# Storing tiles 4 and 5 as a pair in a batched x·yᵀ kernel, with VectorE taking half of their evictions and GpSimd half of one rearrangement

## The chip, the core and the metric

One core of a Trainium2 chip. The metric is the device time of one execution in microseconds, as the median of several runs; the kernel before takes 297.76 us (three runs, 297.63 to 298.08).

## The reference

```python
batch, n_heads, seq_t, seq_s, channels = 8, 12, 512, 512, 64
# x: (batch, n_heads, seq_t, channels), y: (batch, n_heads, seq_s, channels), float32
def reference(x, y):
    return np.einsum('bhtc,bhsc->bhts', x, y).astype(np.float32)
```

For each of 96 heads the result is x times y transposed, 512 x 512, contracted over 64 channels. The inputs are 12.6 MB each, the output is 100.7 MB, all float32.

## The kernel before

**Tiles and groups.** The heads are taken in 6 groups of 16. A group's x and its y are one load each of 2 MB (128 partitions of 16 KB): load 2g is x of group g, load 2g + 1 is y. A group gives two *halves* i = 2g and 2g + 1, and each half gives V = 4 output tiles of 2 MB, 48 tiles in all; tile o belongs to half o // 4.

**Slots.** `room` is 8 slots of 16 KB per partition, in 4 pairs: slots 2n and 2n + 1 are pair n. Loads go to slots 0 to 4 (`places`, line 154), and output tiles go through the same slots. Slots 5, 6 and 7 hold, until they are used for output, the bfloat16 copies of groups 1, 2 and 3 (`xks`, `ybs`, lines 78 to 88): x in the first half of the slot, y in the second. `held` (line 157) makes a tile that goes into such a slot wait for the readers of these copies.

**From a load to a tile.**
- `compress(n)` (line 208) turns load n into bfloat16. An x load is one ScalarE instruction. A y load is four instructions, on VectorE, GpSimd, VectorE and ScalarE (`in_front`; the last y load has GpSimd in the last place).
- `mix(i, engine, part)` (line 231) rearranges the x copy of half i into `xb`, four parts; halves 0, 1 and 2 on GpSimd inside the first loop, later ones on VectorE.
- `transposes(i)` (line 246): two VectorE transposes, `xb` to `xT` and the y copy to `yT`. There are two of each, for even and odd halves; the second instruction tells TensorE that a half is ready (`made`).
- `all_products()` (line 280): TensorE goes through all tiles in order. Each tile is two groups of four 128 x 512 matmuls, one into PSUM buffer `pm0` and one into `pm1` (half of PSUM each). A group waits until its buffer was emptied (`free0`, `free1`).
- `result(o)` (line 390): the two evictions of tile o, `pm0` and `pm1` into the two halves of its slot, on ScalarE (on VectorE for the last tile alone), and then `store(o)`.
- `store(o)` (line 365): tiles 0 to 5 (`o < SINGLE`) are each stored with one 2 MB transfer from slot `alone[o]`. From tile 6 on, an even and an odd tile fill one pair, and the odd one issues one 4 MB transfer for both (line 386). Which pair is used follows `ROUNDS`: 1, 0, 2 in turn for ten pairs of tiles, then all four pairs in turn. The pair of tiles 44 and 45 is stored in parts, and tail work (`shares`, `rest`) follows.

**What sets the order.** Each engine runs its instructions in the order in which the program emits them, and waits on semaphores that `emit` derives from the names read and written. All loads and nearly all stores are issued by SP on one hardware queue, in emission order. The first loop (line 430) runs over loads n = 0 to 11; `load(n + 5)` is issued in turn n for n below 5, loads 10 and 11 in turns 6 and 8. Tiles 0 and 1 come after `compress(8)` and `compress(9)`, tiles 2 and 3 ahead of `compress(10)` and `compress(11)`. Then `prepare(2)` (transposes of half 2, x copies of half 3) and the loop of lines 446 to 449 over the other tiles, with a `prepare` after each fourth one.

Of the kernel before, what the change touches and what calls it, by code (L numbers as in the profile page):

```python
# [9 lines left out]
def kernel(  # L10
# [25 lines left out]
    NH = 2 * NG  # L36
    V = G // 4
# [3 lines left out]
    SLOTS = 5  # L41
    N = K * S
    SINGLE = 2 * V - 2
    SHARED = V * NH - V
    PAIRS = 4
    LATE = 10
    ROUND = [1, 0, 2]
    ROUNDS = [ROUND[n % 3] for n in range(LATE)]
    while len(ROUNDS) < (V * NH - SINGLE) // 2:
        ROUNDS += [PAIRS - 1, *ROUND[LATE % 3:], *ROUND[:LATE % 3]]  # L50
    LAST = 2 * ROUNDS[(V * NH - SINGLE) // 2 - 1]
    CUT = [S, 3 * S]
# [39 lines left out]
    pms = [nc.alloc_psum_tensor(f"pm{i}", [P, 4, S], fp32)[:, :, :] for i in range(2)]  # L92
# [6 lines left out]
    def need(name, points, told=True):  # L99

        best = {}
        for p, v in points:
            if known[name].get(p, 0) < v:
                best[p] = max(best.get(p, 0), v)
        for p, v in list(best.items()):
            if any(snaps[q, w].get(p, 0) >= v for q, w in best.items() if q != p):
                del best[p]
        for p, v in best.items():
            if told:
                engines[name].wait_ge(sems[p], v)  # L110
            known[name][p] = v
            for q, w in snaps[p, v].items():
                known[name][q] = max(known[name].get(q, 0), w)

    def promise(name, reads, writes):

        points = [writer[r] for r in (*reads, *writes) if r in writer]
        points += [v for w in writes for v in readers.get(w, ())]
        if name == "pool" and name in ticks:
            points.append((name, ticks[name]))  # L120
        return points

    def record(name, p, step, reads, writes, queue=False):
        at = (p, ticks.get(p, 0) + step)
        ticks[p] = at[1]
        if not queue:
            own[name][p] = at[1]
        snaps[at] = {**known[name], **own[name], p: at[1]}
        for r in reads:
            readers.setdefault(r, []).append(at)  # L130
        for w in writes:
            writer[w], readers[w] = at, []

    def signal(p):
        if p not in sems:
            sems[p] = nc.alloc_semaphore(p)
        return sems[p]

    def emit(name, make, reads=(), writes=(), dma=None, by=None, step=1):
        need(name, promise(name, reads, writes))  # L140
        p = by or name
        if dma is not None:
            p, step = f"dma{dma}", 16
        made = make().then_inc(signal(p), step)
        record(name, p, step, reads, writes, dma is not None)
        return made.ins.name
# [4 lines left out]
        signal(p)  # L151
    loaded = {}

    places = [0, 1, 2, 4, 3, 0, 1, 2, 4, 3, 1, 4]
    alone = [0, 2, 3, 0, 1, 4]
    heads = [0, 2, 1, 3]
    held = {
        SLOTS + g - 1: [[("xk", g)], [("yb", h, g, ch) for h in range(2) for ch in range(2)]]
# [4 lines left out]
    def copy(name, dst, src, reads, writes, by=None):  # L163
        emit(
            name,
            lambda: nc.scalar.activation(dst, src, COPY)  # L166
            if name == "act"
            else engines[name].tensor_copy(dst, src),  # L168
            reads,
            writes,  # L170
            by=by,
        )

    def both(*ids):
        return [("slot", i, pm) for i in ids for pm in range(2)]
# [7 lines left out]
    def transfer(name, dst, src, to=None, of=None):  # L183

        to = to or dst.ap
        of = of or [src.ap[0], *[[1, 1]] * (len(to) - len(src.ap)), *src.ap[1:]]
        return engines[name].add_instruction(  # L187
            mybir.InstDMACopy(
                name=nc.get_next_instruction_name(),
                engine=engines[name].engine,  # L190
                ins=[place(src, of)],
                outs=[place(dst, to)],
                mode="Copy",
                cce_op=mybir.AluOpType.bypass,
                queue={"sp": "qSPDynamicHW", "pool": "qPoolDynamic"}[name],
            )
        )
# [33 lines left out]
    def mix(i, name, part):  # L231

        g, half = divmod(i, 2)
        ch, u = divmod(part, 2)
        lo = half * 64 + u * D
        xk = g % (NG - 1)
        xv2 = xbs[half].bitcast(bf16).rearrange("p (k e c u) -> p k e c u", k=K, e=E, u=2)
        copy(
            name,
            xv2[part * D:(part + 1) * D, :, :, :, u],  # L240
            xks[xk].rearrange("p (e k c) -> p k e c", e=E, k=K)[lo:lo + D, :, :, ch * D:(ch + 1) * D],
            [("xk", xk)],
            [("xb", half, part)],
        )
# [55 lines left out]
    def shares(o, s):  # L300

        to, mine = ov[o // V, heads[o % V]], slots[s]
        def odd(name, b, e, k, lo, hi):

            p = 4 * e + 32 * b + (32 if e > 7 else 0)
            n = 2 * k
            dst = to[p // 2:p // 2 + n, 1, lo:hi].rearrange("(k i) n -> k i n", i=2)
            part(name, dst, mine[p + 1:p + 2 * n:2, lo:hi], k, both(s), "pool" if name == "pool" else s)

        for b in range(2):  # L310
            for e, k in turns:
                odd("pool", b, e, k, 0, N if e else CUT[b])
        for b in range(2):
            odd("sp", b, 0, 4, CUT[b], N - b * LEFT)
# [10 lines left out]
    def lies(e):  # L325

        return 4 * e + (32 if e > 7 else 0)

    def again():

        half, h = SHARED // V % 2, heads[SHARED % V]
        xT = xTs[half].bitcast(bf16)
# [17 lines left out]
    def rest():  # L350

        half = SHARED // V % 2
        to = ov[SHARED // V, heads[SHARED % V]]
        top = lies(16)
# [10 lines left out]
    def store(o):  # L365
        i, j = divmod(o, V)
        if o == SHARED:
            s = 2 * ROUNDS[(o - SINGLE) // 2]
            shares(o, s)
        elif o == SHARED + 1:  # L370
            n = ROUNDS[(o - SINGLE) // 2]
            emit(
                "sp", lambda: transfer("sp", ow[i, heads[j - 1]][:, :2], pairs[n][::2]),
                reads=both(2 * n, 2 * n + 1), dma=2 * n,
            )
            emit(
                "sp", lambda: transfer("sp", ov[i, heads[j]][:, 1], slots[2 * n + 1][1::2]),
                reads=both(2 * n + 1), dma=2 * n + 1,
            )
        elif o < SINGLE:  # L380
            s = alone[o]
            emit("sp", lambda: nc.sync.dma_start(ov[i, heads[j]], slots[s]), reads=both(s), dma=s)
        elif o % 2:
            n = ROUNDS[(o - SINGLE) // 2]
            emit(
                "sp", lambda: transfer("sp", ow[i, heads[j - 1]], pairs[n]),
                reads=both(2 * n, 2 * n + 1), dma=2 * n,
            )

    def result(o):  # L390

        s = alone[o] if o < SINGLE else 2 * ROUNDS[(o - SINGLE) // 2] + o % 2
        ot = slots[s].rearrange("p (r s) -> p r s", s=S)
        for k in range(0, K, 4):
            pm = k // 4
            half = o // V % 2
            reads, writes = [("xT", half), ("yT", half)], [("pm", pm)]
            signal("pe")
            need("pe", promise("pe", reads, writes), told=False)
            record("pe", "pe", 1, reads, writes)  # L400
            copy(
                "dve" if o == V * NH - 1 else "act", ot[:, k:k + 4, :], pms[pm],
                [("pm", pm)], [("slot", s, pm), *(held[s][pm] if s in held else ())], by=f"free{pm}",
            )
        store(o)

    def prepare(i):

        if i < NH:
            transposes(i)  # L410
        if i + 1 < NH:
            for part in range(4):
                mix(i + 1, "dve", part)


    for n in range(SLOTS):
# [11 lines left out]
            writes=[("xb", half, part) for part in range(4)],  # L428
        )
    for n in range(2 * NG):  # L430
        if n > 9:
            result(n - 8)
        compress(n)
        mix(n // 4, "pool", n % 4)
        if n == 4:
            transposes(0)
        if n < 5:
            load(n + SLOTS)
        elif n in (6, 8):
            load(n // 2 + 7)  # L440
        if n in (8, 9):
            result(n - 8)
        if n == 9:
            transposes(1)
    prepare(2)
    for o in range(V, V * NH):
        result(o)
        if o % V == V - 1:
            prepare(o // V + 2)
    all_products()  # L450
# [38 lines left out]
```

## Time and profile before

| what | value |
|---|---|
| median of runs | 297.76 us |
| profiled execution | 297.92 us |
| its span, first to last instruction | 296.1 us |
| bytes moved | 125.85 MB, 425 GB/s over the span |
| HBM read, written | 25.17 MB, 100.66 MB |
| TensorE matmul busy | 134.9 us (46%) |
| VectorE busy | 157.7 us (53%) |
| ScalarE busy | 205.3 us (69%) |
| GpSimd busy | 64.8 us (22%) |
| ScalarE waiting for a store to land | 31.1 us in 15 waits |
| mean granted TensorE clock | 0.825 |

The engines are PE (TensorE), DVE (VectorE), ACT (ScalarE), POOL (GpSimd) and SP (SyncE, which issues the transfers here). All positions in time are microseconds from the start of the span. A store is "issued" when SP's instruction starts, and it "lands" when the last of its 16 semaphore increments arrives. "L166" and the like are lines of the kernel. In a group's line, the part ahead of the count names what is written and what it is made from.

### The profile page before, as it was taken

What the parts mean: (1) busy time and instruction counts of PE and PEld (TensorE: products, weight loads), DVE (VectorE), ACT (ScalarE), POOL (GpSimd) and SP (SyncE); (2) the same over time, 40 slices, a digit from 0 to 9 for tenths busy, and PEclk for the clock granted to TensorE, in tenths of its full rate; (3) what the DMA queues carried; (4) which work ended last, traced back from release to release, by engine and by line L of the source; (5) the groups of instructions that cost most, each with busy time, mean ns of one, the idle gap of its engine ahead of it and who ended that gap; (6) DMA issues with size and microseconds to landing.
All of it is one profiled execution on the core that took longest, in us unless ns stands there. A gap on an engine that the chain in (4) does not pass through costs nothing.

```text
span 296.1 us, 1221 instructions
## 1 busy us (share of the span) xinstructions
PE 134.9 (46%) x403; PEld 36.9 (12%) x403; DVE 157.7 (53%) x76; ACT 205.3 (69%) x106; POOL 64.8 (22%) x33
## 2 busy tenths in 40 slices
PE   0000040474656575446655866565457755661000
PEld 0000010121111111111111211111111111121000
DVE  2167897896978681935908568772925100052000
ACT  1665666999999978766966999969666966640000
POOL 2399999997000000000000000000000000402000
PEclk9999999996899977887577699977877577877555
DMA  7999999999999999999999999999999999999997
GB/s 286 427 432 432 429 429 427 434 421 427 432 434 445 425 429 435 452 438 434 425 429 422 434 429 447 434 438 429 425 429 425 434 429 447 432 430 430 432 427 305
DMA packets 6042, 125.85 MB, mean 425 GB/s; under 512 B 952, under 2 KB 952, under 8 KB 996
## 3 DMA queue, kind: packets, MB, share of 16 engines
q1 hardware_dynamic: 5656, 124.95, 98.5%
q0 software_dynamic: 384, 0.89, 0.8%
q14 instruction: 2, 0.02, 0.0%
HBM read 25.17 MB, written 100.66 MB: 425 GB/s over the span
## 4 chain that ended last, share of the span: by engine, by line
DMA 56%; ACT 22%; PE 7%; issue 3%; DVE 2%; SPq 1%; POOL 1%; ACTq 0%
DMA out_dram<-room 40%; ACT room L166 21%; DMA room<-in_x_dram 9%; DMA room<-in_y_dram 7%; PE pm L274 6%; DVE yb L168 1%; PE pm L343 1%; ACT xk L166 1%; DVE room L168 1%; SPq L203 1%; POOL out_dram L187 1%; DVE xk L168 0%; ACTq L110 0%
## 5 line engine op out<-in xcount | busy, mean ns | idle before, releaser
L166 ACT ACTIVATE room<-pm 128x2048 f32<-128x2048 f32 x94 | 170.2, 1891 | 34.8 <-DMA out_dram<-room 31.1
L274 PE MATMUL pm<-yT,xT 128*128 128x512 bf16 x384 | 132.0, 488 | 132.2 <-ACT room L166 95.1
L251 DVE STREAM_TRANSPOSE xT<-xb 128x2048 uint32<-128x2048 uint32 x12 | 46.7, 3892 | 59.5 <-PE pm L274 54.7
L274 PEld LDWEIGHTS pm<-yT,xT 128*128 128x128 bf16 x384 | 35.4, 113 | 228.0 <-ACT room L166 147.9
L187 POOL DMA_DIRECT2D out_dram<-room x6 | 3.5, 590 | 180.7 <-ACT room L166 180.7
L168 DVE COPY xb<-room 32x2048 bf16<-32x2048 bf16 x20 | 26.1, 1305 | 0.6
L166 ACT ACTIVATE room<-room 128x4096 bf16<-128x4096 f32 (+1 forms) x6 | 18.3, 3043 | 11.1 <-DMA room<-in_x_dram 7.3
L168 POOL COPY xb<-xk 32x2048 bf16<-32x2048 bf16 x8 | 23.5, 2943 | 6.7 <-ACT xk L166 6.2
L168 DVE CAST yb<-room 64x2048 bf16<-64x2048 f32 x6 | 17.2, 2864 | 9.4 <-DMA room<-in_y_dram 9.3
L168 DVE COPY room<-pm 128x2048 f32<-128x2048 f32 x2 | 4.5, 2286 | 31.9 <-PE pm L274 31.9
L168 DVE CAST room<-room 64x2048 bf16<-64x2048 f32 x6 | 19.1, 3181 | 4.1 <-DMA room<-in_y_dram 4.0
L168 DVE COPY xb<-xk 32x2048 bf16<-32x2048 bf16 x16 | 20.9, 1308 | 0.4
L166 ACT ACTIVATE xk<-room 128x4096 bf16<-128x4096 f32 x3 | 10.9, 3617 | 5.4 <-DMA room<-in_x_dram 5.4
L168 POOL CAST yb<-room 64x2048 bf16<-64x2048 f32 x4 | 12.7, 3186 | 0.5 <-DMA room<-in_y_dram 0.2
L168 POOL COPY xb<-room 32x2048 bf16<-32x2048 bf16 x4 | 12.7, 3174 | 0.3
L260 DVE STREAM_TRANSPOSE yT<-yb 128x1024 uint32<-128x1024 uint32 x6 | 11.6, 1928 | 0.0
L260 DVE STREAM_TRANSPOSE yT<-room 128x1024 uint32<-128x1024 uint32 x6 | 11.5, 1915 | 0.0
L168 POOL CAST room<-room 64x2048 bf16<-64x2048 f32 x3 | 8.6, 2860 | 0.9 <-DMA room<-in_y_dram 0.6
L166 ACT ACTIVATE yb<-room 64x2048 bf16<-64x2048 f32 x2 | 4.9, 2446 | 1.3 <-DMA room<-in_y_dram 1.3
L187 POOL DMA_DIRECT2D out_dram<-xk x3 | 1.7, 572 | 13.1 <-DVE xk L168 13.1
L166 ACT ACT_TABLE_LOAD x1 | 1.3, 1283 | 4.4 <-PEq L419 4.4
L427 DVE MEMSET xb<- 128x2048 uint32 x1 | 1.8, 1765 | 4.8 <-PEq L419 4.8
(8 smaller groups left out, 7.8 us busy)
## 6 DMA issues: line engine op xcount, KB each, us to landing
out_dram<-room SPq DMA_DIRECT2D x20, 4096.0 KB, 24.3
out_dram<-room SPq DMA_DIRECT2D x7, 2048.0 KB, 11.5
room<-in_x_dram SPq DMA_DIRECT2D x6, 2048.0 KB, 18.6
room<-in_y_dram SPq DMA_DIRECT2D x6, 2048.0 KB, 20.8
out_dram<-room SPq DMA_DIRECT2D x1, 1024.0 KB, 29.4
out_dram<-room POOLq DMA_DIRECT2D x2, 256.0 KB, 18.3
out_dram<-room POOLq DMA_DIRECT2D x2, 96.0 KB, 16.6
out_dram<-room SPq DMA_DIRECT2D x1, 112.0 KB
```

The source lines that it names most:

```text
L166: lambda: nc.scalar.activation(dst, src, COPY)
L168: else engines[name].tensor_copy(dst, src),
L187: return engines[name].add_instruction(mybir.InstDMACopy(name=nc.get_next_instruction_name(), engine=engines[name].engine, ins=[place(src, ...
L203: lambda: nc.sync.dma_start(slots[i], (yv if n % 2 else xv)[n // 2]),
L251: lambda: nc.vector.transpose(xTs[half].rearrange("p (k r e) -> p k e r", k=K, e=E), xbs[half].rearrange("p (k e c) -> p k e c", k=K, e=E),),
L260: lambda: nc.vector.transpose(yTs[half].rearrange("p (r j) -> p j r", r=D), ybs[half][b].rearrange("p (j c) -> p j c", c=D),),
L274: last = nc.tensor.matmul(pms[k // 4][:, j, :], xT[:, k + j, h, :], yT[:, h * S:(h + 1) * S], start=True, stop=True,)
L343: last = nc.tensor.matmul(pms[0][:top, at // S, at % S:at % S + hi - lo], xT[:, stop - top:stop], yT[:, h * S + lo % S:h * S + lo % S + hi ...
L427: lambda: engines[name].memset(xbs[half], 0.0),
```

## The change

- Tiles 0 and 1 leave as one pair (pair 0), tiles 2 and 3 alone (from slots 2 and 4), and tiles 4 and 5 as a pair again (pair 0). Before, tiles 0 to 5 each left alone.
- The loads' slots change with this (`places`). Load 11 goes into the slot of load 7, where before it went into the slot of load 8.
- The turn of the pairs is 1, 2, 0 where it was 1, 0, 2, so tiles 8, 9 lie in slots 4, 5 and tiles 10, 11 in slots 0, 1.
- Tiles 0 and 1 are emitted ahead of `compress(8)` and `compress(9)`, in the same place of the loop's turn as tiles 2 and 3.
- VectorE evicts the second half (`pm1`) of tiles 4 and 5.
- `prepare(2)` is emitted after tile 5, where it was emitted ahead of tile 4.
- Of the four x copies of half 3 (emitted by `prepare(2)`), the last two are made by GpSimd.

```diff
     SINGLE = 2 * V - 2
+    ALONE = [2, 3]
+    HELPED = [4, 5]
     SHARED = V * NH - V
     PAIRS = 4
     LATE = 10
-    ROUND = [1, 0, 2]
+    ROUND = [1, 2, 0]
...
-    places = [0, 1, 2, 4, 3, 0, 1, 2, 4, 3, 1, 4]
-    alone = [0, 2, 3, 0, 1, 4]
+    places = [0, 4, 3, 1, 2, 0, 4, 3, 1, 2, 4, 3]
+    first = [0, 1, 2, 4, 0, 1]
...
-        elif o < SINGLE:
-            s = alone[o]
+        elif o in ALONE:
+            s = first[o]
             emit("sp", lambda: nc.sync.dma_start(ov[i, heads[j]], slots[s]), reads=both(s), dma=s)
         elif o % 2:
-            n = ROUNDS[(o - SINGLE) // 2]
+            n = first[o] // 2 if o < SINGLE else ROUNDS[(o - SINGLE) // 2]
             emit(
                 "sp", lambda: transfer("sp", ow[i, heads[j - 1]], pairs[n]),
                 reads=both(2 * n, 2 * n + 1), dma=2 * n,
...
-        s = alone[o] if o < SINGLE else 2 * ROUNDS[(o - SINGLE) // 2] + o % 2
+        s = first[o] if o < SINGLE else 2 * ROUNDS[(o - SINGLE) // 2] + o % 2
...
             copy(
-                "dve" if o == V * NH - 1 else "act", ot[:, k:k + 4, :], pms[pm],
+                "dve" if o == V * NH - 1 or pm and o in HELPED else "act", ot[:, k:k + 4, :], pms[pm],
...
             for part in range(4):
-                mix(i + 1, "dve", part)
+                mix(i + 1, "pool" if i == 2 and part > 1 else "dve", part)
...
     for n in range(2 * NG):
-        if n > 9:
+        if n > 7:
             result(n - 8)
...
-        if n in (8, 9):
-            result(n - 8)
         if n == 9:
             transposes(1)
-    prepare(2)
     for o in range(V, V * NH):
         result(o)
+        if o == HELPED[-1]:
+            prepare(2)
         if o % V == V - 1:
             prepare(o // V + 2)
```

## The prediction

> **What bounds the kernel now.** I read the page's 40 slices first, then the DMA queues, then the busy times by stage.
>
> ```profile
> DMA  7999999999999999999999999999999999999997
> GB/s 286 427 432 432 429 429 427 434 421 427 432 434 445 425 429 435 452 438 434 425 429 422 434 429 447 434 438 429 425 429 425 434 429 447 432 430 430 432 427 305
> ...
> q1 hardware_dynamic: 5656, 124.95, 98.5%
> ```
>
> ```profile
> 2.90:62.40 59.50, 10.31 (x24) 2.77 (x24) 41.81 (x15) 39.98 (x16) 50.02 (x17) 1.00 1.00 426
> 62.40:91.80 29.40, 17.29 (x58) 4.74 (x56) 25.37 (x13) 28.95 (x16) 9.36 (x3) 0.88 1.01 433
> 91.80:250.00 158.20, 95.42 (x280) 25.50 (x280) 84.81 (x47) 126.68 (x71) 0.00 (x0) 0.80 1.00 433
> ```
>
> The last two columns of the second fence are the DMA share and GB/s, for the loads, the six stores of one tile, and the stores in pairs: the share is 1.00, 1.01 and 1.00. The 16 DMA engines never run empty between the first load and the last store, so the bytes set the time. No engine's work matters unless it makes a store late enough for the queue to run dry. So I asked how far each store is issued ahead of that moment. The SP rows of the timeline give the issues of stores 1, 3, 5 and of the first pair (6, 7):
>
> ```profile
> 61.08 0.55 SPq L382 DMA_DIRECT2D out_dram<-room  x1
> 72.11 0.54 SPq L382 DMA_DIRECT2D out_dram<-room  x1
> 79.83 0.54 SPq L382 DMA_DIRECT2D out_dram<-room  x1
> 86.91 0.54 SPq L187 DMA_DIRECT2D out_dram<-room  x1
> ```
>
> The trace's landing times are 62.41 for the last load, then 67.31, 72.15, 76.98, 81.86, 86.81 and 91.75 for the six stores, and 101.61 for pair (6, 7). Each of the four stores shown is issued 4.8 to 7.0 us before everything ahead of it has landed. A landing is seen about 0.5 us after the store's last packet, and the engines turn to the next store over the 0.6 us before that (store 4's first packet starts at 80.76, while store 3's last packet ends at 81.36 and lands at 81.86). So the queue runs dry some 0.8 us before a landing, on the mean of the engines.
>
> How long one tile takes once a slot becomes free is in the chain of waits, around the landing of pair (6, 7):
>
> ```profile
> 86.91 14.70 DMA out_dram<-room
> ...
> 101.69 1.89 ACT room L166
> 103.58 0.05 issue
> 103.62 1.90 PE pm L274 x4
> 105.52 0.02 issue
> 105.54 3.65 ACT room L166 x2
> ```
>
> The landing is at 101.61. The eviction starts 0.08 us later and takes 1.89; the four matmuls of the next tile's first half take 1.90 at the slow clock (1.04 in later groups, where the granted clock is 1.00); a second eviction on the same engine starts 1.77 after the first.
>
> **Part 1: two more pairs.** Tiles 0, 1 and tiles 4, 5 leave in two stores of 4 MB instead of four of 2 MB; the bytes are the same. By landings, six singles take 91.75 - 62.41 = 29.34 us, 4.890 each, 9.78 for two. The 16 pairs from 101.61 to 258.62 take 157.01, 9.81 each. So a pair costs 0.03 more than two singles, 0.07 us for both. The records of single packets say the opposite: 611.5 ns for 16 KB in the singles, 1214 for 32 KB in the pairs, 9 ns less per two, times 256 packets by 16 engines, a gain of 0.15 us. I take +0.07, since landings are what the slots wait for, with bounds -0.15 and +0.07.
>
> **Part 2: ScalarE's new order, and the early stores.** Tiles 0 and 1 are evicted ahead of the compressions of loads 8 and 9. ScalarE ends its share of load 7 at 45.29 and now idles until 47.76. By the rows (1.77 + 1.89 for a tile, 3.62 for an x load, 2.45 for a y share): tile 0 from 45.3 to 49.0, load 8 to 52.6, tile 1 to 56.2, load 9's share to 58.6, tile 2 to 62.3, load 10 to 65.9, tile 3 to 69.5. Inputs are there: tile 0's products run at 36.8, slot 0 is read by VectorE until 43.4, load 8 lands at 47.7, load 9 at 52.6, and each later tile's products come 1.9 us behind an eviction. Issues: pair (0, 1) at 56.2 against a dry queue at 61.6, store 2 at 62.3 against 71.4, store 3 at 69.5 against 76.2. Before, store 0 went out at 54.94; the 1.3 us of delay are covered by load 11, which still lands at 62.41. The last load now waits for load 7's copies, which end on VectorE at 50.33 (before, for load 8's at 51.38); the queue has six microseconds of loads left at that time, so this is worth nothing. Cost of part 2: 0. Past its cover (5.4, 9.1 and 6.7 us) each microsecond would cost one.
>
> **Part 3: the chain of tiles 4 and 5, where it is tight.** Both slots of pair 0 come free together, at 62.41 + 9.81 = 72.2, call it L. Before, slot 0 was free at 67.31 and tiles 4, 5 found free slots 1 and 4. From L the chain is: 0.08 to start; tile 4's first half on ScalarE 1.89, its second half at the same time on VectorE, 2.29; 0.04; tile 5's eight matmuls at the slow clock 3.59 (the row of the first eight, at 36.81); 0.02; tile 5's second half on VectorE 2.29; 0.03 to SP. Sum 7.94: pair (4, 5) is issued at 80.15. Load 0 is the only transfer that meets an empty queue: issued at 0.74, first packet at 1.75, so 1.0 us. First packets at 81.15. Tiles 2 and 3 keep the queue until L + 9.78 = 81.98 by landing, so dry at about 81.15 on the mean, the earliest engines at 80.8. What is lost lies between 0 (first packets before all engines are dry) and 0.35 (none finds work before 81.15, the issue taking 0.54 here against 0.38 for load 0, which adds 0.16); I take 0.12. If the matmuls run at 1.04 per four, the chain is 1.5 us shorter and the loss 0.
>
> The Trainium skill ("DMA: Bandwidth & Descriptors", section Specifications) gives about 0.6 us to the first byte for a transfer from the sync queue. Load 0 shows 1.0, and 0.63 counted from the end of its issue; no store before meets an empty queue. By 0.6 us the loss would be 0 and the sum of all parts 0.07.
>
> The price of VectorE's eviction comes from the end of the kernel, where GpSimd is idle; here GpSimd copies at the same time:
>
> ```profile
> L168 DVE COPY xb<-xk x16: 1279/1306/1335, 161.9 to 215.2; 32x2048 bf16<-32x2048 bf16 x16
> L168 POOL COPY xb<-xk x8: 2440/2942/3480, 12.3 to 45.8; 32x2048 bf16<-32x2048 bf16 x8
> L168 DVE CAST yb<-room x6: 1334/3302/3444, 13.5 to 66.2; 64x2048 bf16<-64x2048 f32 x6
> ...
> L168 DVE COPY room<-pm x2: 2280/2286/2291, 262.6 to 264.8; 128x2048 f32<-128x2048 f32 x2
> ```
>
> ```profile
> L251 DVE STREAM_TRANSPOSE xT<-xb x12: 3874/3894/3908, 31.1 to 225.1; 128x2048 uint32<-128x2048 uint32 x12
> ```
>
> VectorE's casts take 1.33 us alone and 3.44 with GpSimd beside them; its transposes, slower per element, take 3.87 to 3.91 in both settings. An eviction from pm has 1.12 ns per element against the cast's 0.65 and the transpose's 1.9, and I take it as unaffected, 2.29; the other bound is 2.29 x 3.44 / 1.33 = 5.9.
>
> **Part 4: transposes and mixes behind it.** prepare(2) moves behind tile 5 on VectorE: 80.1 to 86.0 (3.9 + 1.95, before it ended at 77.7). Its x copies: two instead of four on VectorE, 2.6 instead of 5.3 us, to 88.6; the other two on GpSimd after its last y work, 72.0 + 2 x 3.4 = 78.8, ten microseconds before the transposes that read them. Tiles 6, 7 need none of this: ScalarE evicts them from 79.9 to 87.5, and pair (6, 7) is issued against a dry queue at 91.0, 3.5 us ahead. Tile 8 needs the transposes of 86.0, which are done. Tile 9 now lies in slot 5, whose second half holds y values that the next transposes read: they run 88.6 to 94.5, so that half is evicted until 96.4 and pair (8, 9) is issued 4.4 us ahead of 100.8. Then tile 11 at 103.6 against 110.6; ScalarE gains on the queue as before. The swapped order of pairs 0 and 2 keeps three pairs in turn. Cost 0; the covers are 3.5 and 4.4 us, beyond which it is paid one for one.
>
> **Sum.** 0.07 + 0 + 0.12 + 0 = +0.2 us, all of it kept to the end because the queue has no slack later. The profiled execution took 297.92 (span 296.1 and 1.8 outside), 0.16 above the median of 297.76; median plus 0.2 is 298.0. About 0.2%, 0.6 us, is what a measurement of this kernel can tell from no change, so I forecast no change that shows: 297.4 to 298.35.
>
> **Rivals.**
> *GpSimd blocks VectorE's evictions (slower).* Tile 4's second half would run 72.3 to 78.2, tile 5's matmuls into that half to 80.0 and its eviction, past GpSimd's copies at 78.8, to 82.3; first packets at 83.4, 2.2 us after the queue is dry: 300.1. For it speak the casts' 1.33 and 3.44; against it the flat transposes. It decides once tile 4's half takes over 4.2 us. Chance 0.12. The Trainium skill ("GPSIMD Engine Reference", section 1) ties this contention to VectorE instructions in a two-port mode or with two SBUF inputs, which an eviction from PSUM is not; no row before shows such an eviction beside GpSimd.
>
> *The queue runs dry before pair (4, 5) for longer than I reckon (slower).* A store may need 1.5 to 2 us from issue to first packet where the load needed 1.0, or each link of the chain 0.1 more; it decides from 0.4 us over my 7.94. With 1.9 us to the first packet the loss is 0.9 and the time 298.75; up to 299.2 with both. For it: the margin is 0 by my sum. Against it: load 0. Chance 0.15.
>
> *Late transposes (slower).* If tile 9's second half or pair (6, 7) comes over 3.5 us late, the overshoot is paid; an overshoot of 1 us gives 299.0. Every term is a row above and the cover is large: 0.04.
>
> *A real gain.* The packet records give at most 0.15; no idle DMA time stands there to be won, so 297.1 or less would need pairs that move faster than any row shows. Chance 0.07.
>
> **How the numbers follow.** Forecast 0.62, slower cases 0.12 + 0.15 + 0.04 = 0.31, faster 0.07. The range takes in the forecast's own and the dry queue's, 297.3 to 299.2; the blocked evictions at 300.1 stay outside.
>
> **What would show it.** DMA share near 1 in every stage but perhaps 80 to 83 us; pair (0, 1) issued near 56.2 and landed at 72.2; VectorE's two new evictions at 2.29 us; pair (4, 5) issued at 80.1. It is wrong if those evictions take over 4 us, if the issue comes after 80.6, or if a gap lies before pair (8, 9).

## The result, and the profile after

The changed kernel takes 298.60 us (7 runs, 298.20 to 299.44) where the kernel before, in the same comparison, takes 297.72 (297.39 to 298.08). The ratio is 1.0034, with a 95% interval of 1.0024 to 1.0044. That is slower by 0.34%, just beyond the 0.2% that I took as the limit of "no change". The profiled execution took 298.51, with a span of 296.4. The 0.88 us have two parts. In the median of the runs the span grew from 295.8 to 296.5. The rest is time outside the span, ahead of the first instruction or behind the last: 2.03 to 2.15 us in every run of the changed kernel, 1.78 to 1.90 in every run of the kernel before whose span is on record.

The page of the changed kernel, its DMA lines:

```profile
span 296.4 us, 1215 instructions
...
DMA  7999999999999999999999999999999999999998
GB/s 279 429 436 431 424 436 427 424 447 407 455 429 424 424 433 443 438 433 433 433 424 421 424 429 429 438 447 438 433 429 424 424 424 429 423 428 418 427 431 354
...
q1 hardware_dynamic: 5368, 124.95, 98.7%
```

The busy times by stage, with the same cuts as before (the last two columns are DMA share and GB/s):

```profile
2.90:62.40 59.50, 12.20 (x28) 3.07 (x28) 41.80 (x15) 42.37 (x17) 49.96 (x17) 0.91 1.00 427
62.40:91.80 29.40, 18.27 (x51) 5.03 (x52) 24.25 (x11) 23.54 (x13) 14.25 (x5) 0.72 1.00 430
91.80:250.00 158.20, 92.32 (x276) 24.91 (x280) 87.91 (x49) 127.19 (x71) 0.00 (x0) 0.83 1.01 432
```

The DMA engines are as busy as before, and there is no hole. The same bytes, 124.95 MB on the hardware queue, in fewer packets (5368 against 5656, from the two new pairs), take 98.7% of a span that is 0.3 us longer. So the engines don't wait; they work longer on the same bytes. That is the part inside the span. The schedule itself came out nearly as worked out. These are VectorE's rows around the pair (4, 5), and SP's issue of it:

```profile
72.32 2.29 DVE L170 COPY room<-pm 128x2048 f32<-128x2048 f32 x1 [2.60 <-DMA out_dram<-room]
77.00 2.29 DVE L170 COPY room<-pm 128x2048 f32<-128x2048 f32 x1 [2.39 <-PE pm L276]
79.32 3.90 DVE L253 STREAM_TRANSPOSE xT<-xb 128x2048 uint32<-128x2048 uint32 x1
```

```profile
79.36 0.54 SPq L189 DMA_DIRECT2D out_dram<-room  x1
```

Both evictions take 2.29 us, the first with GpSimd copying beside it (its row in this trace: 72.16 to 77.16). The pair is issued at 79.36, and the first DMA engine takes it up at 80.78, without a gap.

**Where the time went.** The trace also records every packet. In the records of 32 KB packets (the stores in pairs), in ns:

| | before | changed kernel |
|---|---|---|
| mean of pairs (6, 7) to (12, 13) | 1214.4 | 1216.2 |
| mean from 120 to 245 us, about | 1214.7 | 1219.6 |
| share of those over 1216 ns | 6% | 50% |
| mean of all 32 KB packets | 1215.7 | 1220.6 |

In the changed kernel each engine moves 180 packets of 32 KB, so 4.9 ns make 0.88 us; the mean engine ends 0.95 us later (295.69 against 294.73). It is chance that this equals the difference of the medians: the span ends with the last landing, which in these two traces comes only 0.34 us later. The landings hide the slower packets for a long time. A store lands with its slowest engine, and by the landings that one is no slower than before: pair (6, 7) lands at 101.33 (before 101.61), the pair of tiles 40, 41 at 268.56 (269.02). Only in the last 28 us, where the last pairs of tiles leave in parts, does the lead turn into a loss: 279.11 against 279.18, then 296.36 against 296.02.

So the question for the experiments was what makes packets of the same size, from the same buffers, slower by 0.4% for the rest of a run.

### The profile page after: what moved, and what is told of

The parts are those of the page before. It is cut to its first block, busy times and chain, and to the rows that moved or that the text cites. A ratio compares the mean times of both kernels' runs of the same rounds, so it can differ in the third digit from the quotient of the medians.

```text
span 296.4 us, 1215 instructions
## 1 busy us (share of the span) xinstructions
PE 135.3 (46%) x397; PEld 37.0 (12%) x403; DVE 159.7 (54%) x76; ACT 202.3 (68%) x104; POOL 69.6 (23%) x35
## 3 DMA queue, kind: packets, MB, share of 16 engines
q1 hardware_dynamic: 5368, 124.95, 98.7%
## 4 chain that ended last, share of the span: by engine, by line
DMA 53%; ACT 22%; DVE 6%; PE 6%; issue 3%; POOL 1%; SPq 0%; ACTq 0%
DMA out_dram<-room 40%; ACT room L168 21%; DMA room<-in_y_dram 7%; DMA room<-in_x_dram 6%; PE pm L276 5%; DVE xT L253 3%; DVE room L170 2%; ACT xk L168 1%; PE pm L345 1%; DVE xb L170 1%; DVE yT L262 1%; POOL out_dram L189 1%; DVE xk L170 0%; SPq L205 0%; ACTq L112 0%
## 5 line engine op out<-in xcount | busy, mean ns | idle before, releaser
L168 ACT ACTIVATE room<-pm 128x2048 f32<-128x2048 f32 x92 | 167.1, 1885 | 39.8 <-DMA out_dram<-room 32.1
L170 DVE COPY room<-pm 128x2048 f32<-128x2048 f32 x4 | 9.1, 2289 | 36.9 <-PE pm L276 34.3
L170 DVE COPY xb<-room 32x2048 bf16<-32x2048 bf16 x18 | 23.5, 1305 | 0.5
L170 POOL COPY xb<-room 32x2048 bf16<-32x2048 bf16 x6 | 17.7, 2943 | 0.5
```

## The experiments

"Lead" below is the time from a store's issue to the moment when the first DMA engine has nothing else to do.

### One part at a time

**The kernel before with the new turn of the pairs.**

```diff
-    ROUND = [1, 0, 2]
+    ROUND = [1, 2, 0]
```

> The kernel before with one edit: pairs rotate 1, 2, 0 instead of 1, 0, 2. In the trace after, pair (4, 5) is issued in time and tile 42's store lands 0.07 us earlier than before, yet the end is 0.34 us later and the mean 32 KB packet takes 1220.6 ns against 1215.7. Theory A, the rotation (where the pairs lie while others are written, and which pair the tail uses) slows the packets: 298.5 us, packets near 1220. Theory B, the two early pair stores set the 16 DMA engines' spacing and with it the packets' speed: 297.7, packets near 1215. Theory C, the order of the engines' work (VectorE's evictions, GpSimd's copies): 297.7.

Measured: 298.37 us against 297.68, ratio 1.0027 (1.0017 to 1.0037); packets 1221.0 from 120 to 245 us. It looks like theory A. But the trace shows what the new turn brings about: tiles 8 and 9 now go into slots 4 and 5, slot 4 is occupied by tile 5's store until 91.65, and the pair is issued 5.3 us later than before.

```profile
99.26 0.54 SPq L187 DMA_DIRECT2D out_dram<-room  x1
```

The first engine is idle from 100.16 and the packets come from 100.45 on; seven engines wait, and over the 16 engines 0.11 us are lost in the mean.

**The changed kernel with the old turn of the pairs.**

```diff
-    ROUND = [1, 2, 0]
+    ROUND = [1, 0, 2]
```

> The changed kernel with the old rotation 1, 0, 2. Theory A: 297.7, packets near 1215. Theory B: 298.6, packets near 1220. Theory C: 298.6.

Measured: 298.83 us, ratio 1.0044 (1.0030 to 1.0058); packets 1221.0. Theory A is out: with the old turn the changed kernel is no faster. This trace has a gap too, before pair (4, 5), as the prediction had feared. TensorE's row of tile 5's products and SP's issue:

```profile
74.13 3.31 PE L276 MATMUL pm<-yT,xT 128*128 128x512 bf16 x8 [2.29 <-ACT room L168]
```

```profile
79.84 0.54 SPq L189 DMA_DIRECT2D out_dram<-room  x1
```

The engines run dry from 80.72 on, the first packets of the pair start at 81.03, and over the 16 engines 0.12 us are lost in the mean. Pair (8, 9) is near the limit here too: issued at 99.12, 1.4 us ahead, without a gap.

**The changed kernel without VectorE's and GpSimd's help.**

```diff
-    HELPED = [4, 5]
+    HELPED = []
...
-                mix(i + 1, "pool" if i == 2 and part > 1 else "dve", part)
+                mix(i + 1, "dve", part)
...
+    prepare(2)
     for o in range(V, V * NH):
         result(o)
-        if o == HELPED[-1]:
-            prepare(2)
```

> The changed kernel with ScalarE evicting all of tiles 4 and 5, VectorE making all x copies of half 3, and the transposes of half 2 back ahead of tile 4. From the landing of pair (0, 1) at 72.2, four evictions on ScalarE bring pair (4, 5) to about 79.8, as the changed kernel's 79.4, ahead of the dry queue. Theory A and theory B: 298.6. Theory C: 297.7.

Measured: 298.37 us, ratio 1.0022 (1.0013 to 1.0032); packets 1220.7; pair (4, 5) issued at 79.56, 1.1 us of lead, with gaps of up to 0.2 us on a few engines. Theory C is out. ScalarE alone brings the pair at nearly the same time (79.56) as ScalarE and VectorE together did in the first trace (79.36). Alone, its four evictions run from 72.03 to 79.54 with 0.21 us of waiting; together, VectorE waits until 77.00 for tile 5's products. The span is as long as the changed kernel's, 296.5 in the median; the 0.23 us between the times lie outside it, 1.78 to 1.89 us here.

**The changed kernel with tiles 0, 1, 4, 5 stored alone.**

```diff
-    ALONE = [2, 3]
+    ALONE = [0, 1, 2, 3, 4, 5]
```

> The changed kernel with tiles 0, 1, 4 and 5 stored alone, from the same slots and in the same order of evictions: six stores of 2 MB as in the kernel before. Theory A: 298.6, packets near 1220. Theory B: 297.7, packets near 1215. Theory C: 298.6.

Measured: 298.06 us, ratio 1.0012 (1.0003 to 1.0021); packets 1214.7. Theory B has the packets right, but its time, 297.7, is missed, and it doesn't fit the first run, which has six single stores and slow packets. The span is 296.0 in the median, 0.2 us more than the kernel before's, which stays open, and 2.05 to 2.18 us lie outside it. So the longer time outside the span goes with VectorE's and GpSimd's help and the new place of `prepare(2)`, the only things that the run without help takes back; the pairs have no part in it. Which of the three does it, and how, no run shows. What the three slower kernels share is a store issued at most 1.1 us ahead of the first idle engine. That is theory H of the next four runs.

### A late store by itself

**The kernel before, one store made late.** SP's wait for tile 8's evictions delays the store of pair (6, 7) alone.

```diff
-                reads=both(2 * n, 2 * n + 1), dma=2 * n,
+                reads=both(2 * n, 2 * n + 1, *([0] if o == 7 else [])), dma=2 * n,
...
-        store(o)
+        if o != 7:
+            store(o)
+        if o == 8:
+            store(7)
```

> The kernel before, with the store of pair (6, 7) issued only after tile 8's evictions: near 90.5 where it was 86.9, with first packets 1.2 us later, at 91.7, while the queue runs dry at 90.5 to 91.0. One gap of about 0.9 us, and nothing else is changed. Theory H, a store that meets an empty or nearly empty queue leaves the DMA engines in a slower pattern for the rest of the run: packets near 1220 ns from then on, 0.9 + 0.7 = +1.6 us, 299.3. Theory P, it is the early stores in pairs as such that slow the packets: only the gap is lost, 298.6, packets near 1215.

Measured: 299.01 us against 297.62, ratio 1.0049 (1.0036 to 1.0062); packets 1221.1. SP's issue:

```profile
90.05 0.54 SPq L187 DMA_DIRECT2D out_dram<-room  x1
```

The gap is in the DMA share by stage (a packet counts where it starts, so short stretches scatter), first in the kernel before, for the middle stretch alone, and then in this run:

```profile
90.40:91.20 0.80, 0.72 (x4) 0.31 (x4) 0.80 (x1) 0.80 (x2) 0.00 (x0) 1.00 1.34 574
```

```profile
89.40:90.40 1.00, 0.32 (x2) 0.21 (x3) 1.00 (x2) 1.00 (x2) 0.00 (x0) 1.00 0.84 360
90.40:91.20 0.80, 0.71 (x4) 0.10 (x2) 0.77 (x2) 0.80 (x1) 0.00 (x0) 1.00 0.06 21
91.20:92.20 1.00, 0.35 (x2) 0.21 (x3) 1.00 (x1) 1.00 (x2) 0.00 (x0) 1.00 1.22 524
```

The share is 0.06 for 0.8 us, where it was 1.34. Issued at 90.05, the pair's first packets start at 91.24; by the packet records an engine waits 0.67 us in the mean. The time grew by 1.39, less than the 1.6 expected, since the gap is shorter. The 0.7 us beyond the gap I put down to the slower packets, which begin here and stay to the end, 200 us later, though no other store is late. So in the kernel before, the cause is shown: one store is made late, nothing else is changed, and both effects appear.

**Each of the two new pairs alone.**

```diff
-    ALONE = [2, 3]
+    ALONE = [2, 3, 4, 5]
```

> The changed kernel with tiles 4 and 5 stored alone, tiles 0 and 1 still as a pair. The store of tile 4 is issued near 74.6 and tile 5's near 79, against queues that are dry at 81 and 86, so no store is late. Theory H: packets near 1215 and the time of the run with all six alone, 298.0. Theory P: packets near 1220, 298.5.

```diff
-    ALONE = [2, 3]
+    ALONE = [0, 1, 2, 3]
```

> The changed kernel with tiles 0 and 1 stored alone, tiles 4 and 5 still as a pair. Slot 0 is free at 67.5 and slot 1 at 72.4, so the pair is issued near 74.8, six microseconds ahead. Theory H: packets near 1215, 298.0. Theory P: packets near 1220, 298.5.

Measured: 297.85 us, ratio 1.0007 (0.9998 to 1.0015), packets 1214.9, for the first; 297.91 us, ratio 1.0011 (1.0002 to 1.0019), packets 1214.8, for the second. In the second, pair (4, 5) was issued at 78.21, not at 74.8 as expected, which still is 2.5 us of lead. Pairs as such do not slow the packets; theory P is out. The 0.2 to 0.3 us by which these runs are longer than the kernel before lie outside the span again: the spans are 295.7 and 295.8 in the median, the kernel before has 295.8.

### The changed kernel's own spread

**The changed kernel again, for further traces.** No edit.

> The changed kernel once more, for a second trace. By the slow matmuls pair (4, 5) should be issued at 80.1 in most runs and the engines wait up to 0.3 us; by the first trace at 79.4, without a wait. Theory H: the slower the matmuls of tile 5 in the trace, the longer the run; 298.6, packets near 1220.

> The changed kernel, one more trace. In the two traces so far tile 5's eight matmuls took 1.90 us (pair (4, 5) issued at 78.4, packets 1216.8 ns, 297.69 us) and 2.72 us (issued at 79.4, packets 1220.6, 298.51). Theory H: near 3.5 us of matmuls or an issue after 79.4 goes with packets near 1221 and 298.5 or more; 1.9 us of matmuls goes with 297.7. Theory N, the two levels have nothing to do with this store: no such link.

> The changed kernel, a fourth trace, with the same expectation: issue near 78.4 with 297.7, issue from 79.4 on with 298.5 or more (theory H); no link (theory N).

Measured: 298.60 us in the median of seven runs, ratio 1.0028 (1.0017 to 1.0039). But the seven are 297.69 and 297.84, and then 298.50 to 298.88, and two single executions gave 297.65 and 297.83. The three new traces all belong to the lower group, so the upper one has a single trace, the first. TensorE's row of tile 5's products, in the first trace of the changed kernel:

```profile
74.24 2.72 PE L276 MATMUL pm<-yT,xT 128*128 128x512 bf16 x8 [2.33 <-ACT room L168]
```

and in the second, with its issue of pair (4, 5):

```profile
74.05 1.90 PE L276 MATMUL pm<-yT,xT 128*128 128x512 bf16 x8 [2.19 <-ACT room L168]
```

```profile
78.35 0.54 SPq L189 DMA_DIRECT2D out_dram<-room  x1
```

The third and fourth have 1.90 us as well. The same eight instructions take 1.90 us or 2.72, and with the old turn of the pairs 3.31, by where TensorE's granted clock changes. In the three traces with 1.90 it is 1.00 from 72.3 to 72.5 us on; in the first it is 1.00 from 71.76 and falls to 0.50 at 75.17, in the midst of the eight; with the old turn it is 0.50 until 77.01. The Trainium skill ("TensorE: Matmul & The Clock Gate", Part 1) says that the clock is decided in a free-running window of about 3.4 us, so that the number of slow matmuls changes from run to run; the records of the granted clock agree, with changes that lie 3.41 us or multiples of it apart.

| run | tile 5's products, us | late store's lead, us | mean gap, us | packets 120 to 245 us, ns | this trace's run, us |
|---|---|---|---|---|---|
| changed, third trace | 1.90 | 2.2 | 0 | 1215.0 | 297.65 |
| changed, second | 1.90 | 2.4 | 0 | 1215.1 | 297.69 |
| changed, fourth | 1.90 | 2.1 | 0 | 1215.3 | 297.83 |
| changed, first | 2.72 | 1.4 | 0 | 1219.6 | 298.51 |
| no help | 3.42 | 1.1 | 0.03 | 1220.7 | 298.24 |
| old turn | 3.31 | 0.9 | 0.12 | 1221.0 | 298.80 |
| before, new turn | | 0.9 | 0.11 | 1221.0 | 298.43 |
| before, one late | | 0.35 | 0.67 | 1221.1 | 299.01 |

The link that theory N denies is there in all four traces of the changed kernel, but with one trace of the upper group against three of the lower.

### How late, and how often

**The kernel before, the store of pair (6, 7) two microseconds ahead.**

```diff
-                reads=both(2 * n, 2 * n + 1), dma=2 * n,
+                reads=[*both(2 * n, 2 * n + 1), *([("slot", 0, 0)] if o == 7 else [])], dma=2 * n,
...
+            if o == 8 and pm == 0:
+                store(7)
-        store(o)
+        if o != 7:
+            store(o)
```

> The kernel before, with the store of pair (6, 7) issued after tile 8's first eviction: near 88.3, two microseconds ahead of the first engine that runs dry at 90.4, and without a gap. Theory H with a limit between 1.4 us (slow, first trace of the changed kernel) and 2.4 us (fast, its second): 2.1 us ahead should still be fast, 297.7, packets near 1215; if it is slow, 298.3 and near 1220, the limit lies above 2.1 us. Theory P2, any store out of its old turn slows the packets: 298.3.

Measured: 297.77 us, ratio 1.0006 (0.9997 to 1.0015), but in two groups: six runs from 297.49 to 297.77 and five from 298.10 to 298.27. Issued at 88.41, 2.0 us ahead. In its trace (a run of 297.65, so one of the lower group; no run of the upper one was traced) the packets are as before until about 210 us, and then grow to 1218 ns from 230 to 250 us. Theory P2's 298.3 fits the five runs, but not the six. So there is no sharp limit between 1.4 and 2.4 us of lead; with less lead the slower packets start earlier, and with a gap they start at once. The packets that start from 250 to 260 us put all traces in one order, by the lead of the late store. They take 1215.3 to 1218.8 ns where no store is late (the kernel before, the runs with tiles 4 and 5 alone), 1222.3 with a lead of 2.5 us, 1230.2 to 1232.9 with 2.4 to 2.1, 1240.5 with 2.0, and 1242 to 1246 with 1.4 or less. So even the traces of the changed kernel's lower group are not free of it.

**The kernel before, two late stores.**

```diff
-                reads=both(2 * n, 2 * n + 1), dma=2 * n,
+                reads=both(2 * n, 2 * n + 1, *{7: [0], 9: [5]}.get(o, [])), dma=2 * n,
...
-        store(o)
+        if o in (8, 11):
+            store({8: 7, 11: 9}[o])
+        if o not in (7, 9):
+            store(o)
```

> The kernel before with two late stores: pair (6, 7) as in the run with one, and pair (8, 9) issued only after tile 11's evictions, near 100.7, against a queue dry at 101. Theory H, the slower pattern is a state that one late store sets and a second does not deepen: only a second gap of about 0.8 us on top of the 299.0 of one, 299.8, packets near 1221 to 1224 as with one. If every late store adds its own slowing: 299.0 + 0.8 + 0.7 = 300.5, packets near 1228.

Measured: 299.81 us against 297.59, ratio 1.0072 (1.0059 to 1.0086); packets 1221.0. The share of the second gap:

```profile
100.90:101.70 0.80, 0.67 (x4) 0.10 (x1) 0.80 (x1) 0.28 (x1) 0.00 (x0) 1.00 0.10 41
```

The two gaps sum to 1.31 us per engine, against 0.67 with one; the time grew by 0.80 over the run with one late store, and the packets are no slower. So far as one run of it goes, the slower pattern is a state that the first late store sets and a second does not deepen.

**What stays open.** Why the packets are slower in that state. After the gap of the run with one late store, all 16 engines start within 0.15 us of each other, and the packets after these take 1241 to 1252 ns; so it seems that they get in each other's way. In the runs with a gap the engines also stay closer together: from 120 to 245 us a packet has 3.9 to 5.0 other packets that start within 50 ns of it, and 1.1 to 3.3 in the runs without a gap. But the third trace of the changed kernel has 3.3 and packets of 1215.0 ns, the first has 2.5 and packets of 1219.6, and within a run this distance does not separate slow packets from fast ones. So I don't claim it.

## Why the prediction was right and where it was wrong

The time fell into the range, 297.3 to 299.2, but the forecast was 298.0 and "no change that shows", and the kernel is slower by more than the bound. The range reaches to 299.2 because of the rival of a dry queue, whose reason was another than the one that the runs showed. So it is luck that the time lies inside.

- *Part 1, pairs against singles:* right as far as it can be measured. In the trace after, the two new pairs take 9.69 and 9.71 us by landings and the two singles between them 9.71, so there is neither the price of 0.07 nor a clear gain. The spans don't decide it: 296.0 with no early pair, 295.7 and 295.8 with one, 295.6 to 295.8 in the three traces of the lower group with both.
- *Part 2, the early stores:* right. Issues at 56.4, 62.6 and 70.0 against the 56.2, 62.3 and 69.5 worked out, and pair (0, 1) landed at 72.22 against 72.2.
- *Part 3, the chain of tiles 4 and 5:* the place was right, and the chain too, as far as its clock. I took 3.59 us for tile 5's products; they took 1.90 to 3.42, and the pair came 78.4 to 79.8 where I had 80.15. From issue to first packet it took 1.19 to 1.20 us in the five traces with a gap (I had 1.0 from load 0, plus up to 0.16). The Trainium skill's 0.6 us ("DMA: Bandwidth & Descriptors", Specifications) agrees if one counts from the end of the 0.54 us issue: 0.65. The waiting that I priced at 0.12 us is 0.12 in the trace with the old turn.
- *The term that failed* is the price of a late store in this part, "what is lost lies between 0 and 0.35". I counted the engines' waiting alone. What a late store costs beyond it is the slower packets to the end of the run, some 0.7 us by the run with one late store, even where no engine waits at all (lead 1.4 us in the first trace). With that, the sum would have been 0.9 and the forecast "slower". In the changed kernel itself this rests on the four traces of the table and on the runs that take the late store away, not on a run that changes its lead alone.
- *A second term was put at nothing without a reason:* the sum took the 1.8 us outside the span as fixed. They became 2.03 to 2.15, some 0.25 us of the 0.88. In the traces of the changed kernel's lower group a shorter span, 295.6 to 295.8 us, against 295.8 before, makes up for a part of it. Why the time outside the span grew stays open.
- *Part 4, transposes and mixes:* right. They ended at 85.0, pair (8, 9) was issued at 95.3, and no later store was late.
- *Rivals.* GpSimd blocking VectorE's evictions fell: 2.29 us for both, the first of them wholly beside GpSimd's copies. The Trainium skill ("GPSIMD Engine Reference", section 1) ties this contention to VectorE instructions in a two-port mode or with two SBUF inputs; the 2.29 us agree with it. What spoke for this rival was a misreading: the cast of 1.33 us (52.66 to 53.99 in the trace before) did not run alone, a cast of GpSimd ran beside it from 52.77 on, and so the ratio 3.44 / 1.33 and the bound of 5.9 show nothing of GpSimd. "The queue runs dry for longer" named the right store, and its 298.75 was near the time, but its reason, a slower start of the store, was not the one: the start took 0.2 us more than load 0's where it could be seen, and in the trace after no engine waited. Late transposes and a real gain did not appear.

## What to carry to other kernels

In a kernel like this one, whose DMA queue never runs dry, the price of a store that comes too late is not the hole alone: look at the duration of the packets after it. Work out for each store how far it is issued ahead of the moment when the first engine runs out of work, and don't be content with zero: here a lead of 2.5 us was nearly free and one of 1.4 us was not; a margin that hangs on TensorE's clock differs from run to run, so look at the single times for two groups. And when a change costs time without a hole, compare packet durations before and after, since landings can stay the same until the end. Compare the span and the time outside it separately, too.

## What the runs showed of the hardware

- After a store with a lead of 1.4 us or less, 32 KB packets took 1219.6 to 1221.1 ns from 120 to 245 us in place of 1214.7.
- From SP's issue to the first packet of a store on an idle engine: 1.19 to 1.20 us, in five traces.
- VectorE evicts 128x2048 float32 from PSUM in 2.29 us also while ScalarE evicts the other buffer and GpSimd copies.
- The same matmuls at the same place of the same kernel took 1.90 or 2.72 us in different executions; the three runs with 1.90 took 297.65 to 297.83 us and the one with 2.72 took 298.51.
- The time outside the span was 1.78 to 1.90 us without VectorE's and GpSimd's help and 2.03 to 2.18 with it, in every run.
